# The projection of the values as seven products of halves instead of eight

## The chip, the cores and the metric

The kernel runs on one core of a Trainium2 chip. The core has a matrix engine (TensorE, PE in the profile), a vector engine (VectorE, DVE), an engine for activations and copies (ScalarE, ACT), a general one (GpSimd, POOL) and a queue for loads (SyncE, SP); POOL and ACT can issue transfers too. Each engine works off its own list of instructions in order and waits for the others by semaphores. The metric is the device time of one execution in microseconds; less is better.

## The reference

One layer of an encoder over 512 tokens of 1024 features, in float32. After a layer norm the tokens `h` are multiplied by one wide matrix `w_in`, whose columns give queries, keys and values of a 2-D neighbourhood attention (16 heads of 64), the inputs of a bidirectional state-space mixer (SSD), and two gates:

```
h = layer_norm(x)                         # 512 x 1024
proj = h @ w_in                           # columns: q | k | v | z | x,B,C | dt | gates
q, k, v, ... = split(proj)                # v: 512 x 1024, columns 2048..3071 of w_in
ya = neighbourhood_attention(q, k, v, rpb) @ w_attn_br   # 8 x 64 grid, window 8 x 16
ys = ssd(...) @ w_ssd_br
h = layer_norm(a * h + (sigmoid(g0) * ya + sigmoid(g1) * ys) @ w_o)
out = layer_norm(a * h + square(relu(h @ w_ff1)) @ w_ff2)
```

What is changed is how `v`, that is h (512 x 1024) times 1024 columns of w_in, is computed.

## The kernel before

**Products in float32.** Each float32 operand is kept as two parts, a high one (rounded to the matmul's format) and a low one (the remainder). `mm3` (L404 to L406) multiplies high by high, low by high and high by low, three matmuls for each 128 x 128 by 128 x 512 piece. Weights come in slabs of 1 MB (`ws`, loaded by SP, two buffers); ACT copies the high part (`wh`, L386), DVE subtracts for the low part (`wl`, L387), each in two halves of 128 x 1024, and `wh` and `wl` have two buffers each, too. The layer norm leaves the tokens as `hTh` and `hTl`, high and low, features on the partitions.

**Stages.** Layer norm and SSD come first; their order is laid out by a planner (class Plan), which assigns times and writes every engine's list out. Its last work is SSD branch 7: eight outputs `ps_sbr7_0` to `_7` in the two PSUM banks "mm", each emptied by DVE into the sum `ysacc` (L1104). From there on the order is set by the framework's scheduler, which places the instructions by the waits it sees. Then come the projection of the values, attention, the two branches with their gates, the output projection, and the FFN. The FFN's second matrix is multiplied with seven products of halves already; there POOL issues plain loads (L1559) and adding loads (L1570, a DMA that adds what it reads onto what lies in the slab).

**The projection of the values.** The tokens are first copied into another order, blocks of neighbourhood columns (`hBh`, `hBl`, 128 x 512 each, eight on ACT at L1186, eight on DVE at L1188). Then for each half of the 1024 columns (s) four PSUM banks, one for each block of 128 tokens, gather eight steps of 128 features: 2 x 4 x 8 x 3 = 192 matmuls of 128 x 512, over four slabs `ws_v`. The result leaves PSUM as high and low parts `vhl` (ACT L1202, DVE L1203).

**Attention** goes through eight pairs of heads. For each pair a slab `ws_qk` (two loads of 512 KB) is split, q and k are projected (`ps_q`, `ps_k`), copied out (`qf`, L1233; `kf`, L1246) and parted into `qs` (ACT L1238, POOL L1241), `kh` and `klz` (DVE L1249, POOL L1251). For each head eight small loads bring the relative biases (`raw`, L1262), which POOL turns into `bias` (L1267, L1271). Scores `pss` are added to the bias on DVE (`sc`, L1289), exponentiated on ACT (L1295), scaled (L1299), transposed on PE (`tp_p`, L1310) and multiplied with `vhl` (`po`, L1323). POOL also multiplies the gates `gt` with `ysacc` at the start of this stage (L1419).

## Time and profile before

| what | us |
|---|---|
| median of 3 runs (lowest, highest) | 1177.96 (1176.69, 1182.29) |
| the profiled execution | 1179.89 |
| its span, first to last instruction | 1178.1 |
| projection of the values on PE | 496.4 to 540.3 |
| PE busy | 1159.9 (98%) |
| DVE, ACT, POOL busy | 761.0, 615.0, 545.6 |
| mean granted clock of PE | 0.996 of full speed |

The profile is of one execution. A row of the timeline or of the chain of waits gives start, duration, engine, line, operation, output <- inputs, how many in a row, and in brackets the idle time before and what ended it. A row of a group of instructions gives the shortest, median and longest duration in ns, and the starts of the first and the last. A row of a stage gives busy time and count of each engine, then PE's granted clock, the mean busy share of the 16 DMA engines and what they moved in GB/s.

### The profile page before, as it was taken

To read this page: it belongs to the slowest core of one execution; us is meant where nothing else is said; L and a number is where in the kernel's file an instruction comes from. 1 tells how busy PE (TensorE), PEld (TensorE's weight loads), DVE (VectorE), ACT (ScalarE), POOL (GpSimd) and SP (SyncE) were. 2 spreads that over 40 slices of the span, in tenths; PEclk is the share of its full clock that TensorE was granted. 3 is DMA by queue.
4 is the path that set the end of the run, shared out by engine and by line. 5 is a ranking of instruction groups with operands and counts; after the bars stand their busy time and mean duration, and the time that the engine had idled before them with its cause. 6 is when DMAs were issued, how large, how long until landed. Compare 5 with 4: busy or idle time off the path is not lost.

```text
span 1178.1 us, 17062 instructions
## 1 busy us (share of the span) xinstructions
PE 1159.9 (98%) x6442; PEld 982.9 (83%) x6442; DVE 761.0 (65%) x1363; ACT 615.0 (52%) x1033; POOL 545.6 (46%) x588
## 2 busy tenths in 40 slices
PE   8999999999999999999999999999999999999997
PEld 8978797879888888888888888888988888878886
DVE  7757475676766665434788975556552666498856
ACT  6577583836365564524667773342263554365410
POOL 1168968778788767204667630016055131221000
PEclk9999999999999999999999999999999999999999
DMA  6353333333333342233423313543237986779511
GB/s 202 94 162 126 107 126 108 124 110 126 107 108 115 120 142 69 75 107 87 101 70 90 86 37 107 179 170 117 72 108 201 248 194 184 189 207 228 160 52 53
DMA packets 129409, 149.22 MB, mean 127 GB/s; under 512 B 22960, under 2 KB 101808, under 8 KB 129328
## 3 DMA queue, kind: packets, MB, share of 16 engines
q1 hardware_dynamic: 115696, 112.63, 30.8%
q0 software_dynamic: 13056, 34.61, 12.2%
q8 instruction: 50, 0.82, 0.3%
q10 hardware_dynamic: 576, 0.92, 0.2%
q14 instruction: 31, 0.25, 0.1%
HBM read 145.90 MB, written 2.23 MB: 126 GB/s over the span
## 4 chain that ended last, share of the span: by engine, by line
PE 83%; DMA 6%; DVE 5%; ACT 2%; issue 2%; POOL 2%; SPq 1%; DVEq 0%; POOLq 0%; ACTq 0%
PE ps_f L404 8%; PE ps_f L406 8%; PE ps_f L405 8%; PE ps_x L404 4%; PE ps_x L406 4%; PE ps_x L405 4%; PE ps_abr L1373 4%; PE ps_sbr L404 2%; DMA w2r<-in_w_ff 2%; PE ps_z L404 2%; PE ps_sbr L406 2%; PE ps_z L405 2%; PE ps_z L406 2%; PE ps_sbr L405 2%; PE ps_g L405 2%; PE ps_g L404 2%
## 5 line engine op out<-in xcount | busy, mean ns | idle before, releaser
L787 DVE SCALAR_TENSOR_TENSOR cv<-ps_x,pc,cv 128x511 f32<-128x511 f32 (+1 forms) x128 | 95.7, 748 | 24.7 <-ACT cv L779 21.4
L405 PE MATMUL ps_f<-h1Th,wl_f 128*128 128x512 f32 (+1 forms) x288 | 104.0, 365 | 0.0
L404 PE MATMUL ps_f<-h1Th,wh_f 128*128 128x512 f32 (+1 forms) x288 | 103.6, 365 | 0.0
L406 PE MATMUL ps_f<-h1Tl,wh_f 128*128 128x512 f32 (+1 forms) x288 | 102.0, 365 | 0.0
L1576 DVE TENSOR_TENSOR wl_f<-w2r,wh_f 128x1024 fp32r<-128x1024 f32 x42 | 49.9, 1221 | 64.4 <-ACT wh_f L1575 64.1
L404 PE MATMUL ps_z<-wh_z,hTh 128*128 128x256 f32 x256 | 75.2, 294 | 0.0
L405 PE MATMUL ps_z<-wh_z,hTl 128*128 128x256 f32 x256 | 71.5, 279 | 0.0
L406 PE MATMUL ps_z<-wl_z,hTh 128*128 128x256 f32 x256 | 71.5, 279 | 0.0
L1570 POOL DMA_DIRECT2D w2r<-in_w_ff x30 | 36.3, 1416 | 70.7 <-DMA w2r<-in_w_ff 45.7
L405 PE MATMUL ps_f<-wh_f,sql 128*128 128x512 f32 x168 | 65.3, 390 | 0.9 <-DVE sql L1576 0.9
L1575 ACT ACTIVATE wh_f<-w2r 128x1024 fp32r<-128x1024 f32 x42 | 42.6, 1052 | 44.0 <-DMA w2r<-in_w_ff 32.6
L404 PE MATMUL ps_f<-wh_f,sqh 128*128 128x512 f32 x168 | 65.3, 391 | 0.3 <-ACT sqh L1575 0.3
L406 PE MATMUL ps_f<-wl_f,sqh 128*128 128x512 f32 x168 | 65.3, 390 | 0.1
L1104 DVE TENSOR_TENSOR ysacc<-ps_sbr,ysacc 128x512 f32<-128x512 f32 x56 | 38.5, 689 | 37.5 <-PE ps_sbr L406 37.1
L404 PEld LDWEIGHTS ps_f<-h1Th,wh_f 128*128 128x128 f32 x288 | 53.9, 188 | 9.0
L405 PEld LDWEIGHTS ps_f<-h1Th,wl_f 128*128 128x128 f32 x288 | 53.9, 188 | 8.7
L387 DVE TENSOR_TENSOR wl_f<-ws_f,wh_f 128x1024 fp32r<-128x1024 f32 x36 | 47.2, 1348 | 20.5 <-ACT wh_f L386 20.4
L406 PEld LDWEIGHTS ps_f<-h1Tl,wh_f 128*128 128x128 f32 x288 | 52.8, 188 | 8.6
L404 PE MATMUL ps_x<-hTh,wh_bc 128*128 128x512 f32 (+1 forms) x144 | 56.7, 394 | 0.5 <-ACT hTh L614 0.5
L404 PE MATMUL ps_sbr<-yTh,wh_sbr 128*128 128x512 f32 x128 | 55.7, 435 | 0.7 <-ACT yTh L1081 0.4
L406 PE MATMUL ps_x<-hTl,wh_bc 128*128 128x512 f32 (+1 forms) x144 | 53.5, 371 | 1.9 <-DVE hTl L629 1.9
L404 PE MATMUL ps_x<-hTh,wh_x 128*128 128x512 f32 (+1 forms) x144 | 54.6, 379 | 0.0
(346 smaller groups left out, 3724.0 us busy)
## 6 DMA issues: line engine op xcount, KB each, us to landing
ws_f<-in_w_ff SPq DMA_DIRECT2D x20, 1024.0 KB
w2r<-in_w_ff POOLq DMA_DIRECT2D x18, 1024.0 KB, 7.9
bc<-acs_d SPq DMA_DIRECT2D x32, 512.0 KB
w2r<-in_w_ff POOLq DMA_DIRECT2D x30, 512.0 KB, 9.4
ws_bc<-in_w_in SPq DMA_DIRECT2D x16, 512.0 KB
ws_x<-in_w_in SPq DMA_DIRECT2D x8, 1024.0 KB
ws_z<-in_w_in SPq DMA_DIRECT2D x8, 1024.0 KB
ws_g<-in_w_in SPq DMA_DIRECT2D x8, 1024.0 KB
```

The costliest lines, as they stand in the source:

```text
L387: (eng[i] if isinstance(eng, tuple) else eng).tensor_tensor(out=lo[:, k], in0=st[:, k], in1=hi[:, k].bitcast(F32), op=ALU.subtract)
L404: nc.tensor.matmul(o, lh, rh, start=start, stop=False)
L405: nc.tensor.matmul(o, ll, rh, start=False, stop=False)
L406: return nc.tensor.matmul(o, lh, rl, start=False, stop=stop)
L787: op("DVE", 0.75, lambda j=j, o=o, n=n: nc.vector.scalar_tensor_tensor(out=acc()[:, o], in0=ps()[:, n], scalar=tap(j), in1=acc()[:, o], op ...
L1104: op("DVE", 0.69, lambda d=d, ps=ps: nc.vector.tensor_tensor(out=ysacc[:, d, :], in0=ps(), in1=ysacc[:, d, :], op=ALU.add), r=[(ps.name, 0 ...
L1373: ins.append(nc.tensor.matmul(pss[j], u, v, start=k + p == 0, stop=k == KD - 1 and p == 2))
L1570: nc.gpsimd.dma_start(t, rows(i, n, c, k), accum_op=ALU.add)
L1575: nc.scalar.activation(hi[:, k], x, AF.Copy)
L1576: low = nc.vector.tensor_tensor(out=lo[:, k], in0=x, in1=hi[:, k].bitcast(F32), op=ALU.subtract)
```

## The change

The tokens are cut into two halves i (the left and the right 32 columns of the 64-column grid) and two halves of the 1024 features; the weights into two halves of the features and two of the columns. Instead of eight products of such halves, seven are made, each of 256 tokens by 512 features by 512 columns: 2 x 4 x 3 = 24 matmuls of 128 x 512, 168 in all. They run in the order 1, 2, 5, 3, 6, 7, 4.

What they need is made on the chip. **Tokens:** POOL adds high and low parts of the four quarters (L1256 of the changed file), DVE forms the differences (L1268, L1283, L1285, L1300) in the memory of `aT`, and `tokens` parts them into high (ACT, L1217) and low (DVE, L1221), three buffers `vt`. **Weights:** the slab `ws_vsum` is loaded with block 01; adding DMAs of POOL (L1193, two of 512 KB each time) make 01 + 00, later + 11, later + 10, each time after the sum before has been split; block 01 is added onto `ws_v22`. SP loads four slabs as before; the adds read 4 MB more. **Results:** ACT copies the first product (L1278); the others are added on DVE (L1239, fourteen of 128 x 512), and ACT (L1246) and DVE (L1247) part them into `vhl`, now from SBUF. `behind` adds two explicit orderings. The copies hBh and hBl are gone. Everything that follows in the program text is the same.

```diff
 
     hb = tc.tile_pool(name="hb", bufs=1, reuse_waits="tile")
     hbp = hb.__enter__()
-    hBh = hbp.tile([P, KD, S], F32R, name="hBh")
-    hBl = hbp.tile([P, KD, S], F32R, name="hBl")
-    blk = "p (r b j) -> p b r j"
-    for k in range(KD):
-        for src, dst in ((hTh, hBh), (hTl, hBl)):
-            d4 = dst[:, k, :].rearrange("p (b r j) -> p b r j", r=8, b=4)
-            s4 = src[:, k, :].bitcast(F32).rearrange(blk, r=8, b=4)
-            if k < 4:
-                nc.scalar.activation(d4, s4, AF.Copy)
-            else:
-                nc.vector.tensor_copy(d4, s4)
-    for s in range(2):
-        pss = [psx.tile([P, 512], F32, tag=tag, bufs=BANKS[tag], name=f"ps_v{s}_{b}")
-               for b, tag in enumerate(("so", "tr", "so", "tr"))]
-        for k0 in (0, 4):
-            wv = weights([(w_in, k0 * P, OFF_V + s * 512, 512)], 4, 512, f"v{s}_{k0}")
-            for b in range(4):
-                bs = slice(b * P, (b + 1) * P)
-                for k in range(k0, k0 + 4):
-                    mm3(pss[b], hBh[:, k, bs], hBl[:, k, bs], wv[0][:, k - k0, :], wv[1][:, k - k0, :],
-                        k == 0, k == KD - 1)
-        for b in range(4):
-            pv4 = pss[b].rearrange("p (r h q) -> p r h q", r=4, h=2)
-            hi = vhl[s][:, b, :, 0:4:3, :]
-            vdone = nc.scalar.activation(hi, pv4, AF.Copy)
-            nc.vector.tensor_tensor(out=vhl[s][:, b, :, 1:3, :], in0=pv4, in1=hi.bitcast(F32),
-                                    op=ALU.subtract)
-
+
+    def project_values():
+        full = app.tile([P, 4, 4, 256], F32, tag="aT", name="v_full")
+
+        def block(i, n):
+            return w_in[i * 512 : (i + 1) * 512, OFF_V + n * 512 : OFF_V + (n + 1) * 512].rearrange(
+                "(k p) c -> p k c", p=P)
+
+        def load(name, i, n):
+            t = wp.tile([P, 4, 512], F32, tag="ws", name=f"ws_v{name}")
+            nc.sync.dma_start(t, block(i, n))
+            return t
+
+        def plus(t, i, n):
+            for k in (slice(0, 2), slice(2, 4)):
+                nc.gpsimd.dma_start(t[:, k], block(i, n)[:, k], accum_op=ALU.add)
+
+        def split(name, t, after=None):
+            hi, lo = [wide(wp.tile([P, 2112], F32R, tag=n, name=f"{n}_v{name}"), 4) for n in ("wh", "wl")]
+            for k in (slice(0, 2), slice(2, 4)):
+                x = nc.scalar.activation(hi[:, k], t[:, k], AF.Copy)
+                if after is not None:
+                    behind(x, after, "the tokens of the product before")
+                nc.vector.tensor_tensor(out=lo[:, k], in0=t[:, k], in1=hi[:, k].bitcast(F32),
+                                        op=ALU.subtract)
+            return hi, lo
+
+        def quarter(t, i, kk):
+            v = t[:, kk * 4 : kk * 4 + 4, :].bitcast(F32).rearrange("p k (r c) -> p k r c", r=8)
+            return v[:, :, :, i * 32 : i * 32 + 32]
+
+        high, low = {}, {}
+
+        def tokens(name, parts):
+            t = hbp.tile([P, 2, 4, 256], F32R, tag="vt", bufs=3, name=f"vt_{name}")
+            for b in range(2):
+                d = [t[:, n, :, b * P : (b + 1) * P].rearrange("p k (r j) -> p k r j", r=8)
+                     for n in range(2)]
+                hi, *rest = [x[:, :, :, b * 16 : b * 16 + 16] for x in parts]
+                done = nc.scalar.activation(d[0], hi, AF.Copy)
+                if rest:
+                    nc.scalar.activation(d[1], rest[0], AF.Copy)
+                else:
+                    low[name] = nc.vector.tensor_tensor(out=d[1], in0=hi, in1=d[0].bitcast(F32),
+                                                        op=ALU.subtract)
+            high[name] = done
+            return t
+
+        def product(pss, t, w):
+            for j in range(2):
+                for k in range(4):
+                    js = slice(j * P, (j + 1) * P)
+                    mm3(pss[j], t[:, 0, k, js], t[:, 1, k, js], w[0][:, k, :], w[1][:, k, :],
+                        k == 0, k == 3)
+
+        def two(name, *tags):
+            return [psx.tile([P, 512], F32, tag=tag, bufs=BANKS[tag], name=f"ps_v{name}_{j}")
+                    for j, tag in enumerate(tags)]
+
+        def add(out, x, pss, sign=1.0):
+            for j in range(2):
+                nc.vector.scalar_tensor_tensor(out=out[:, j], in0=pss[j], scalar=sign, in1=x[:, j],
+                                               op0=ALU.mult, op1=ALU.add if sign > 0 else ALU.subtract)
+
+        def values(s, half, src, after=None):
+            for j in range(2):
+                v4 = src[:, j].rearrange("p (r h q) -> p r h q", r=4, h=2)
+                hi = vhl[s][:, 2 * half + j, :, 0:4:3, :]
+                done = nc.scalar.activation(hi, v4, AF.Copy)
+                x = nc.vector.tensor_tensor(out=vhl[s][:, 2 * half + j, :, 1:3, :], in0=v4,
+                                            in1=hi.bitcast(F32), op=ALU.subtract)
+                if after is not None:
+                    behind(x, after, "the tokens of the product before")
+            return done
+
+        f21, f22, f11, f12 = [full[:, n].rearrange("p k (r c) -> p k r c", r=8) for n in range(4)]
+
+        def full_sum(f, i, kk):
+            return nc.gpsimd.tensor_tensor(out=f, in0=quarter(hTh, i, kk), in1=quarter(hTl, i, kk),
+                                           op=ALU.add)
+
+        full_sum(f22, 1, 1)
+        full_sum(f21, 1, 0)
+        w11 = load("11", 0, 0)
+        wsum = load("sum", 0, 1)
+        plus(wsum, 0, 0)
+        w21 = load("21", 1, 0)
+        t11 = tokens("11", [quarter(x, 0, 0) for x in (hTh, hTl)])
+        b11 = split("11", w11)
+        t12 = tokens("12", [quarter(x, 0, 1) for x in (hTh, hTl)])
+        nc.vector.tensor_tensor(out=f22, in0=f22, in1=f21, op=ALU.subtract)
+        s1 = tokens("s1", [f22])
+        full_sum(f11, 0, 0)
+        full_sum(f12, 0, 1)
+        p1 = two("1", "so", "so")
+        product(p1, t11, b11)
+        b21 = split("21", w21)
+        w22 = load("22", 1, 1)
+        sums = gep.tile([P, 2, 512], F32, tag="gt", bufs=4, name="v_sums")
+        for j in range(2):
+            nc.scalar.activation(sums[:, j], p1[j], AF.Copy)
+        p2 = two("2", "tr", "tr")
+        product(p2, t12, b21)
+        u1 = split("u1", wsum)
+        plus(wsum, 1, 1)
+        nc.vector.scalar_tensor_tensor(out=f22, in0=f22, scalar=-1.0, in1=f11, op0=ALU.mult,
+                                       op1=ALU.subtract)
+        nc.vector.scalar_tensor_tensor(out=f12, in0=f22, scalar=-1.0, in1=f12, op0=ALU.mult,
+                                       op1=ALU.subtract)
+        s4 = tokens("s4", [f12])
+        p5 = two("5", "mm", "mm")
+        product(p5, s1, u1)
+        b22 = split("22", w22)
+        plus(w22, 0, 1)
+        s2 = tokens("s2", [f22])
+        c11 = gep.tile([P, 2, 512], F32, tag="gt", bufs=4, name="v_c11")
+        add(c11, sums, p2)
+        u2 = split("u2", wsum, high["s4"])
+        plus(wsum, 1, 0)
+        p3 = two("3", "cb", "yd")
+        product(p3, s4, b22)
+        values(0, 0, c11, low["s4"])
+        nc.vector.tensor_tensor(out=f21, in0=f11, in1=f21, op=ALU.subtract)
+        s3 = tokens("s3", [f21])
+        u3 = split("u3", w22)
+        p6 = two("6", "so", "so")
+        product(p6, s2, u2)
+        t22 = tokens("22", [quarter(x, 1, 1) for x in (hTh, hTl)])
+        u4 = split("u4", wsum)
+        c12, c22 = [full[:, n].rearrange("p k c -> p (k c)").rearrange("p (j c) -> p j c", j=2)
+                    for n in (0, 3)]
+        add(sums, sums, p6)
+        add(c22, sums, p5)
+        add(c12, c22, p3, -1.0)
+        p7 = two("7", "tr", "tr")
+        product(p7, s3, u3)
+        values(1, 0, c12)
+        p4 = two("4", "so", "so")
+        product(p4, t22, u4)
+        add(c22, c22, p7, -1.0)
+        add(sums, sums, p7)
+        values(1, 1, c22)
+        add(sums, sums, p4)
+        return values(0, 1, sums)
+
+    vdone = project_values()
     hb.__exit__(None, None, None)
     at = tc.tile_pool(name="at", bufs=1, reuse_waits="tile")
     atp = at.__enter__()
```

The scheduler orders what follows the SSD anew. Three places are shown; the names after `<-` are the inputs, and a row with x2 stands for two of the kind in a row.

POOL from the last weight split of the SSD (`wl_sbr7`) on, before:

```order
L516 TENSOR_TENSOR wl_sbr7_4704<-ws_sbr7_4436,wh_sbr7_4695 128x1024 x2
L1213 MEMSET klz_5122 128x1024
L1419 TENSOR_TENSOR gt0_1_4748<-gt0_1_4748,ysacc_71 128x512 x2
L1267 TENSOR_TENSOR bias0_5224<-raw0_5215,cst_81 128x128
L1271 TENSOR_TENSOR bias0_5224<-raw0_5215,cst_81 128x128
L1267 TENSOR_TENSOR bias0_5224<-raw0_5215,cst_81 128x128
L1271 TENSOR_TENSOR bias0_5224<-raw0_5215,cst_81 128x128
L1241 TENSOR_TENSOR qs0_5160<-qf0_5158,qs0_5160 64x128 x3
```

and now:

```order
L516 TENSOR_TENSOR wl_sbr7_4704<-ws_sbr7_4436,wh_sbr7_4695 128x1024 x2
L1193 DMA ws_vsum_4857<-in_w_in 128x2x512 x2
L1256 TENSOR_TENSOR v_full_4852<-hTh_69,hTl_70 128x1024 x4
L1193 DMA ws_vsum_4857<-in_w_in 128x2x512 x2
L1193 DMA ws_v22_4919<-in_w_in 128x2x512 x2
L1193 DMA ws_vsum_4857<-in_w_in 128x2x512 x2
L1331 MEMSET klz_5174 128x1024
L1385 TENSOR_TENSOR bias0_5276<-raw0_5267,cst_81 128x128
L1389 TENSOR_TENSOR bias0_5276<-raw0_5267,cst_81 128x128
L1385 TENSOR_TENSOR bias0_5276<-raw0_5267,cst_81 128x128
L1389 TENSOR_TENSOR bias0_5276<-raw0_5267,cst_81 128x128
L1537 TENSOR_TENSOR gt0_1_4748<-gt0_1_4748,ysacc_71 128x512 x2
```

Between the last SSD split and the clearing of `klz` stand eight adding DMAs and four sums, and the first head's bias stands ahead of the two products with the gates instead of behind them.

DVE around the end of the SSD, where `ysacc` empties the last branch, before:

```order
L1104 TENSOR_TENSOR ysacc_71<-ps_sbr7_0_4772,ysacc_71 128x512
L387 TENSOR_TENSOR wl_v0_0_4875<-ws_v0_0_4876,wh_v0_0_4874 128x1024
L1104 TENSOR_TENSOR ysacc_71<-ps_sbr7_1_4780,ysacc_71 128x512
L387 TENSOR_TENSOR wl_v0_0_4875<-ws_v0_0_4876,wh_v0_0_4874 128x1024
L1104 TENSOR_TENSOR ysacc_71<-ps_sbr7_2_4788,ysacc_71 128x512
L1104 TENSOR_TENSOR ysacc_71<-ps_sbr7_3_4796,ysacc_71 128x512
L1104 TENSOR_TENSOR ysacc_71<-ps_sbr7_4_4804,ysacc_71 128x512
L1104 TENSOR_TENSOR ysacc_71<-ps_sbr7_5_4812,ysacc_71 128x512
L1104 TENSOR_TENSOR ysacc_71<-ps_sbr7_6_4820,ysacc_71 128x512
L1104 TENSOR_TENSOR ysacc_71<-ps_sbr7_7_4828,ysacc_71 128x512
L1188 CAST hBh_4852<-hTh_69 128x512
L1188 CAST hBl_4853<-hTl_70 128x512
```

and now:

```order
L1104 TENSOR_TENSOR ysacc_71<-ps_sbr7_0_4772,ysacc_71 128x512
L1201 TENSOR_TENSOR wl_v11_4869<-ws_v11_4855,wh_v11_4868 128x1024
L1104 TENSOR_TENSOR ysacc_71<-ps_sbr7_1_4780,ysacc_71 128x512
L1201 TENSOR_TENSOR wl_v11_4869<-ws_v11_4855,wh_v11_4868 128x1024
L1104 TENSOR_TENSOR ysacc_71<-ps_sbr7_2_4788,ysacc_71 128x512
L1104 TENSOR_TENSOR ysacc_71<-ps_sbr7_3_4796,ysacc_71 128x512
L1104 TENSOR_TENSOR ysacc_71<-ps_sbr7_4_4804,ysacc_71 128x512
L1104 TENSOR_TENSOR ysacc_71<-ps_sbr7_5_4812,ysacc_71 128x512
L1104 TENSOR_TENSOR ysacc_71<-ps_sbr7_6_4820,ysacc_71 128x512
L1104 TENSOR_TENSOR ysacc_71<-ps_sbr7_7_4828,ysacc_71 128x512
L1268 TENSOR_TENSOR v_full_4852<-v_full_4852 128x1024
L1201 TENSOR_TENSOR wl_v21_4914<-ws_v21_4861,wh_v21_4913 128x1024 x2
```

The two halves of the first slab's low part (`wl_v11` for `wl_v0_0`) stand at the same places between the evictions; behind them differences of tokens and the next split take the place of the copies.

SP from the loads of the q/k slabs on, before:

```order
L378 DMA ws_qk0_5126<-in_w_in 128x8x128 x2
L378 DMA ws_qk1_5371<-in_w_in 128x8x128 x2
L378 DMA ws_qk2_5616<-in_w_in 128x8x128 x2
L1262 DMA raw0_5215<-in_rpb_pad 16x8x32 x8
L1262 DMA raw1_5292<-in_rpb_pad 16x8x32 x8
L1262 DMA raw2_5460<-in_rpb_pad 16x8x32 x8
L378 DMA ws_qk3_5861<-in_w_in 128x8x128 x2
```

and now:

```order
L378 DMA ws_qk0_5178<-in_w_in 128x8x128 x2
L378 DMA ws_qk1_5423<-in_w_in 128x8x128 x2
L378 DMA ws_qk2_5668<-in_w_in 128x8x128
L1380 DMA raw0_5267<-in_rpb_pad 16x8x32 x8
L1380 DMA raw1_5344<-in_rpb_pad 16x8x32 x8
L1380 DMA raw2_5512<-in_rpb_pad 16x8x32 x8
L378 DMA ws_qk2_5668<-in_w_in 128x8x128
L378 DMA ws_qk3_5913<-in_w_in 128x8x128 x2
```

The second half of `ws_qk2` has moved behind the 24 loads of `raw`.

## The prediction

> **What bounds the kernel now.** I read the page's table of engines first, then the busy time by stage, the instructions of the projection, and the chain of waits where that stage begins.
>
> ```profile
> span 1178.1 us, 17062 instructions
> PE 1159.9 (98%) x6442; PEld 982.9 (83%) x6442; DVE 761.0 (65%) x1363; ACT 615.0 (52%) x1033; POOL 545.6 (46%) x588
> ...
> core 0: us, PE busy (x) PEld busy (x) DVE busy (x) ACT busy (x) POOL busy (x), PEclk, DMA share, GB/s
> 485.00:496.40 11.40, 11.33 (x50) 8.89 (x49) 6.92 (x9) 6.75 (x11) 0.00 (x0) 1.00 0.29 93
> 496.40:540.30 43.90, 43.90 (x195) 36.38 (x194) 17.38 (x24) 12.34 (x16) 0.00 (x0) 1.00 0.33 96
> ...
> L404 PE MATMUL ps_v<-wh_v,hBh x64: 389/389/389, 496.6 to 539.4; 128*128 128x512 f32 x64
> L406 PE MATMUL ps_v<-wl_v,hBh x64: 389/389/389, 497.7 to 539.9; 128*128 128x512 f32 x64
> ```
>
> TensorE (PE) is busy for 98% of the span, and in the projection (496.4 to 540.3) for all of it at the full granted clock, while POOL does nothing, DVE 17.4 us and the DMA engines a third of what they could. The stage is 192 matmuls in a row. So a matmul less is a gain of its whole pitch, and anything that makes PE wait is a loss of its whole length: there is no slack on PE to hide it in. What lies just ahead of the stage is the place that matters here:
>
> ```profile
> 486.78 0.69 DVE L1104 TENSOR_TENSOR ysacc<-ps_sbr,ysacc 128x512 f32<-128x512 f32 x1 [5.82 <-PE ps_sbr L406]
> 487.39 1.22 DVE L387 TENSOR_TENSOR wl_v<-ws_v,wh_v 128x1024 fp32r<-128x1024 f32 x1
> 488.52 0.69 DVE L1104 TENSOR_TENSOR ysacc<-ps_sbr,ysacc 128x512 f32<-128x512 f32 x1
> 489.12 1.22 DVE L387 TENSOR_TENSOR wl_v<-ws_v,wh_v 128x1024 fp32r<-128x1024 f32 x1
> 490.25 1.40 DVE L1104 TENSOR_TENSOR ysacc<-ps_sbr,ysacc 128x512 f32<-128x512 f32 x2
> ...
> 490.25 0.69 DVE ysacc L1104
> 490.99 0.50 PE ps_sbr L404
> ```
>
> The last SSD branch (eight outputs through two PSUM banks) is emptied by DVE, and the first two halves of the V weights' low parts stand between those evictions in DVE's queue. In the chain (the last two rows) PE's fifth output starts at 490.99, right behind the eviction of the third (490.25 + 0.69): PE already waits for DVE there. Whatever delays DVE between 487 and 491 goes on the path at once.
>
> **The change part by part.** *Fewer matmuls.* 192 become 168. The pitch, from the first matmul of L404 to the last of L406, is (539.9 - 496.6) / 191 = 0.2267 us. 24 x 0.2267 = **-5.44 us**. That is 0.46% of 1178, and nothing else is removed from the path, so 5.4 is the most that the change can bring.
>
> *POOL gets work where it had none, beside DVE.* In the new order POOL goes, behind its last weight split, to two adding DMAs (weight block 00 onto 01) and then to four sums hTh + hTl of 128x1024 (L1256 of the changed file). When?
>
> ```profile
> 474.77 4.75 POOL L516 TENSOR_TENSOR wl_sbr<-ws_sbr,wh_sbr 128x1024 fp32r<-128x1024 f32 x2 [0.98 <-ACT wh_sbr L512]
> 540.38 0.95 POOL L1213 MEMSET klz<- 128x1024 f32 x1 [60.87 <-PE ps_v L406]
> 479.54 11.19 SPq L378 DMA_DIRECT2D ws_v<-in_w_in  x2
> 483.00:484.00 1.00, 1.00 (x6) 0.84 (x5) 0.00 (x0) 0.00 (x0) 0.00 (x0) 1.00 0.85 330
> 484.00:485.00 1.00, 1.00 (x7) 0.81 (x6) 0.00 (x0) 0.00 (x0) 0.00 (x0) 1.00 0.02 6
> L1570 POOL DMA_DIRECT2D w2r<-in_w_ff x30: 1177/1228/1729, 896.3 to 1084.6; - x30
> DMA to landing us min/median/max: 6.0/9.4/18.0
> L516 POOL TENSOR_TENSOR wl_z<-ws_z,wh_z x16: 2375/2406/2417, 42.1 to 433.3; 128x1024 fp32r<-128x1024 f32 x16
> L1104 DVE TENSOR_TENSOR ysacc<-ps_sbr,ysacc x56: 673/692/693, 177.9 to 496.8; 128x512 f32<-128x512 f32 x56
> ```
>
> POOL is free from 479.5. The slab that is added onto takes the place of today's second V slab: issued at 479.54, its bytes stop at about 484.2 (330 GB/s in the second before 484, then 6). Two issues of 1.23 us each (the FFN's adding DMAs, L1570) bring POOL to 486.7, and the four sums, 2.4 us each by L516, fill 486.7 to 496.3: exactly the stretch of the DVE rows above. Do the two engines disturb each other? The nearest case is in the FFN:
>
> ```profile
> 867.74 22.81 POOL L1700 TENSOR_TENSOR acc<-acc,row 128x1024 f32<-128x1024 f32 x8 [53.49 <-ACT r L1683]
> 869.84 4.72 DVE L387 TENSOR_TENSOR wl_f<-ws_f,wh_f 128x1024 fp32r<-128x1024 f32 x2 [1.97 <-ACT wh_f L386]
> ```
>
> Two DVE subtractions of the shape of wl_v took 4.72 us beside POOL's additions, where each wl_v above takes 1.22; and POOL's eight took 22.8 where 8 x 2.41 = 19.3. So both lose, and the loss is about the other's work. The evictions ysacc, whose one input is PSUM, never took over 0.693 us in 56 cases, many of them beside POOL's splits: they aren't touched. Taken as turns, an operation waiting until the other engine's is through: POOL's first sum 486.7 to 489.1; the first wl_v (wanted 487.4) 489.1 to 490.3; the eviction of the second output 490.3 to 490.9; POOL's second sum starts at 490.3 behind wl_v and lasts to 492.7; the second wl_v 492.7 to 493.9; the eviction of the third output to 494.6 instead of 490.94. PE's fifth output, and all behind it, starts **+3.6 us** later. If they only shared the rate, each wl_v would last twice as long, 2 x 1.2 = +2.4. Bounds: 0, if the two don't meet (the slab lands over 5 us later, or the sums are short), and 4.8, two whole sums. I take 3.6, since the rows show waiting of about that kind.
>
> [...]
>
> *The adding DMAs.* Eight of 512 KB, in pairs. Call T the start of the first product on PE; a product is 24 x 0.2267 = 5.44 us, and they run 1, 2, 5, 3, 6, 7, 4. The second add (block 11) can start when the sum slab's first split is done, about T + 7.9; its result is wanted by product 6 at T + 21.8. The third (block 10) waits for the next split of that slab, which stands on DVE behind the tokens of products 3, 2 and 7: about T + 21.5, and product 4 wants it at T + 32.7, less one ACT half (1.05) and the start of it: a landing within 9.8 us costs nothing. The add onto 22 has T + 13.1 to T + 27.2. The FFN's adds landed after 6.0 to 18.0 us, median 9.4, at a DMA share far above the 0.33 of this stage; there the first half of a pair is near the minimum. I take **0**, with bounds 0 and what 18 us would give (rival C).
>
> *DVE's load.* From T to the low part of the first q/k weights it has 18 operations of 128x1024 and 21 of 128x512. By the starts above (487.39 to 488.52, 488.52 to 489.12) these follow at 1.13 and 0.60: 20.3 + 12.6 = 32.9 us, against 168 x 0.2267 = 38.1 us of PE. It fits, with 5 us to spare; before, DVE was busy for 17.4 us of 43.9. ACT has less. **0**, bounds 0 and 2 for a late operand.
>
> *The handover to attention.* Two orders change: on SP the second half of ws_qk2 now stands behind the 24 small loads of raw, and on POOL the first bias stands ahead of the two gt multiplications.
>
> ```profile
> 540.07 12.29 SPq L1262 DMA_DIRECT2D raw<-in_rpb_pad  x24
> 552.46 6.53 SPq L378 DMA_DIRECT2D ws_qk<-in_w_in  x4
> 546.86 0.46 POOL L1267 TENSOR_TENSOR bias<-raw,cst 128x128 f32<-128x128 f32 x1 [0.93 <-DMA raw<-in_rpb_pad]
> 548.66 4.21 POOL L1241 TENSOR_TENSOR qs<-qf,qs 64x128 fp32r<-64x128 f32 x10
> 551.81 2.01 ACT L386 ACTIVATE wh_qk<-ws_qk 128x1024 fp32r<-128x1024 f32 x2
> 558.48 0.42 DVE L1289 CUSTOM_DVE_ANT_0 sc<-pss,bias 128x256 f32<-128x256 f32 x1 [0.51 <-PE pss L1285]
> 562.51 1.14 DVE L1299 TENSOR_SCALAR sc<-sc,sums 128x256 f32<-128x256 f32 x4
> 566.88 0.77 PE tp_p L1310 x7
> ```
>
> The first softmax is ready at 563.65 and PE transposes it at 566.88: 3.2 us of slack. After the change raw goes out some 2.3 us later measured from the end of the projection, the 12.3 us of its issues stand ahead of half a q/k slab, so ACT's wh_qk and the eviction behind it come 4 to 6.7 us later and the first score 3.3 us later; PE has, by the new order, five more q matmuls (5 x 0.2267 = 1.1 us) ahead of the transpose. 3.3 against 3.2 + 1.1 leaves nothing or a little: **+0.5**, bounds 0 and 3 (if PE, which waits for ACT here already, can't fill with q).
>
> Sum: -5.44 + 3.6 + 0 + 0 + 0.5 = **-1.3 us**. The profiled execution took 1179.89 (span 1178.1 and 1.8 around it), so it would take 1178.6; it lies 1.9 over the median of the runs, 1177.96, which would become **1176.6**.
>
> **Rivals.** *B, the whole gain.* The sums and DVE's splits don't meet: 1177.96 - 5.44 + 0 to 0.5 = 1172.5 to 1173. For it: the slab's landing is only known to a microsecond or so, and a part of DVE's wait may be there already. Against it: the 4.72 us row, and that the sums last 9.6 us in a stretch of which DVE's splits need the first four.
>
> *C, slower: the add on block 10 comes late.* If a pair lands as the FFN's first four did, up to the 18.0 us of the row, say 10 for the first half and 15 for the second: block 11's second half goes out at T + 9.1, lands at T + 24.3, and is split by T + 26.6 (1.05 + 1.22) instead of the T + 23.6 at which its first low part is wanted, 3.0 us of waiting; block 10's goes out 3.0 late at T + 25.7, lands at T + 40.7, split at T + 43.0 against T + 34.5 + 3.0: 5.5 more. 1176.6 + 8.5 = 1185.1. It decides from a second half's landing of about 10 us. For it: the median of 9.4 lies just under that point, and the q/k slabs load at the same time. Against: 4 MB in 40 us beside a share of 0.33, and pairs alone.
>
> *D, the handover costs 3:* -5.44 + 3.6 + 3 = +1.2, 1179.1. For it, the q/k weights behind 24 loads; against, the slack of 3.2.
>
> **How the numbers follow.** A (the sum) 0.50; B 0.24; C 0.13; D 0.13. What a measurement of this kernel can tell from no change is about 0.5%, 5.9 us: below 1172.1 is faster, above 1183.9 slower. A and D lie within it. B lies half a microsecond inside, and the runs before spread over 1176.69 to 1182.29, so four in ten of B count as faster, and a little of A: 0.11. C counts as slower nearly whole, with a little of D: 0.14. Same 0.75. The range takes B from 1172.0 and reaches up to 1183.0, half way from D to C, since C's price grows steadily with the landing.
>
> **What would show it.** (1) ps_v: 168 matmuls, 0.2267 apart, if no wait lies between; a row of PE waiting for ACT or DVE behind an add's landing is C. (2) The two wl_v11 rows (L1201) between the ysacc rows: 2.4 us and more from the ysacc before to their end, the first ps_v matmul about 500.2; at 496.6, B. (3) L1256: four operations of 2.4 us, stretched by about 1.2 each for the first two. (4) The first score's start against the projection's end, 18.2 us before (558.48 - 540.3): 21.5 forecast; PE's wait ahead of tp_p. The prediction is wrong if T moves by less than 1 or over 5 us, or if PE waits over 1 us between products.

## The result: slower, and the loss lies ahead of the projection

The changed kernel takes 1185.71 us (median of six runs, 1183.77 to 1188.03), the kernel before 1178.22 on the same chip: a ratio of 1.0061 with a 95% interval of 1.0047 to 1.0074, some 7 us more. Forecast were 1176.6, with a range up to 1183.0. The profiled execution of the changed kernel took 1185.6 us with a span of 1183.6.

The page of the changed kernel, its list of what PE waited for between 480 and 760, and the first group of matmuls of the projection and its last one:

```profile
span 1183.6 us, 17096 instructions
PE 1156.8 (98%) x6418; PEld 981.5 (83%) x6418; DVE 791.4 (67%) x1387; ACT 627.9 (53%) x1053; POOL 564.2 (48%) x600
...
PE ps_sbr L404 <- DVE ysacc L1104: 9.4, 1, 9.4
PE tp_p L1428 <- DVE sc L1417: 1.5, 1, 1.5
PE po L1441 <- ACT qf L1351: 0.4, 1, 0.4
...
L404 PE MATMUL ps_v<-wh_v,vt x16: 389/389/389, 507.8 to 518.0; 128*128 128x512 f32 x16
...
545.68 0.39 PE L406 MATMUL ps_v<-wl_vu,vt 128*128 128x512 f32 x1
```

Three things are to be seen. The projection begins at 507.8 instead of 496.6. Its last matmul starts at 545.7 and takes 0.39 us, so it ends at 546.1 instead of 540.3 and lasts 38.2 us instead of 43.7: it does bring what it was to bring. And in it PE waits for nothing: both waits of any size lie outside, one before it (9.4 us, for an eviction of the last SSD branch), one in attention. What happened ahead of it stands in the timelines of POOL and of DVE:

```profile
485.06 2.63 POOL L1193 DMA_DIRECT2D ws_vsum<-in_w_in  x2 [5.73 <-DMA ws_vsum<-in_w_in]
486.80 10.13 POOL L1256 TENSOR_TENSOR v_full<-hTh,hTl 128x1024 f32<-128x1024 f32 x4
...
486.59 0.69 DVE L1104 TENSOR_TENSOR ysacc<-ps_sbr,ysacc 128x512 f32<-128x512 f32 x1 [5.82 <-PE ps_sbr L406]
487.20 10.82 DVE L1201 TENSOR_TENSOR wl_v<-ws_v,wh_v 128x1024 fp32r<-128x1024 f32 x1
497.94 0.68 DVE L1104 TENSOR_TENSOR ysacc<-ps_sbr,ysacc 128x512 f32<-128x512 f32 x1
498.54 1.21 DVE L1201 TENSOR_TENSOR wl_v<-ws_v,wh_v 128x1024 fp32r<-128x1024 f32 x1
```

One subtraction of DVE takes 10.82 us instead of 1.22. It began 0.4 us behind the first of POOL's four sums and ended 1.1 us, about its own length, behind the last (486.80 + 10.13 = 496.93). The eviction queued behind it came 9.6 us late, measured from the eviction before it. The second wl_v, with POOL done, took 1.21 again. What PE lost besides is in the granted clock, the last number but two of each row (the columns are as in the prediction's table by stage):

```profile
487.20:498.60 11.40, 2.07 (x10) 1.38 (x8) 11.40 (x4) 4.77 (x9) 9.72 (x5) 0.76 0.54 93
498.60:503.70 5.10, 5.03 (x12) 3.98 (x13) 2.44 (x4) 0.00 (x0) 0.00 (x0) 0.53 0.55 169
503.70:507.80 4.10, 4.10 (x19) 3.38 (x18) 2.08 (x3) 0.00 (x0) 0.00 (x0) 1.00 0.12 45
508.00:546.20 38.20, 38.20 (x170) 31.62 (x170) 34.55 (x41) 24.35 (x33) 7.25 (x7) 1.00 0.78 165
```

Behind the wait PE ran at about half its clock: 12 matmuls in the 5.1 us after 498.6, which at 0.2267 us each would be 2.7. So 9.4 of waiting and 2.4 of low clock, less some 0.5 us that PE lost at this place before the change too (48 matmuls in 11.36 us, which at 0.2267 would be 10.88), make up the 11.4 us by which the projection starts late.

To compare profiles, whose earlier stages differ by a microsecond or two, I take the first eviction of branch 7 as zero (486.78 before, 486.59 after). The first matmul of the projection then comes at 9.8 before and 21.2 after, and the first of the next stage, ps_abr, at 209.9 and 218.2. So the loss is 8.3 us by the end of attention: +11.4 ahead of the projection, -5.4 in it, and 2.3 in attention. In this pair of profiles the rest gave 2.6 of it back (first before, then changed):

```profile
L1373 PE MATMUL ps_abr<-aTh,wh_abr x64: 389/389/398, 696.7 to 742.8; 128*128 128x512 f32 x64
L404 PE MATMUL ps_f<-h1Th,wh_f x288: 276/389/395, 832.0 to 1120.2; 128*128 128x512 f32 x112, 128*128 128x256 f32 x32
```

```profile
L1491 PE MATMUL ps_abr<-aTh,wh_abr x64: 389/389/397, 704.8 to 750.8; 128*128 128x512 f32 x64
L404 PE MATMUL ps_f<-h1Th,wh_f x288: 276/389/395, 840.1 to 1125.7; 128*128 128x512 f32 x112, 128*128 128x256 f32 x32
```

From ps_abr to the last ps_f of this line it is 423.5 us before and 420.9 after, though nothing was changed in the program text there; in the runs below it is 421 to 426. In the profile of before PE waits 1.2 us for operands of the FFN (ps_f) that it does not wait for in the changed kernel's; how much of the rest is variation from one execution to another, a single profile of each does not show. So spans of single profiles are not compared here to less than 3 us.

### The profile page after: what moved, and what is told of

Read it like the earlier page. It is cut to its first block, busy times and chain, and to the rows that moved or that the text cites. A ratio compares the mean times of both kernels' runs of the same rounds, so it can differ in the third digit from the quotient of the medians.

```text
span 1183.6 us, 17096 instructions
## 1 busy us (share of the span) xinstructions
PE 1156.8 (98%) x6418; PEld 981.5 (83%) x6418; DVE 791.4 (67%) x1387; ACT 627.9 (53%) x1053; POOL 564.2 (48%) x600
## 4 chain that ended last, share of the span: by engine, by line
PE 84%; DVE 5%; DMA 4%; ACT 2%; issue 2%; SPq 1%; POOL 1%; DVEq 0%; ACTq 0%; POOLq 0%
PE ps_f L404 9%; PE ps_f L405 9%; PE ps_f L406 9%; PE ps_x L404 4%; PE ps_x L406 4%; PE ps_x L405 4%; PE ps_abr L1491 4%; PE ps_sbr L404 2%; PE ps_sbr L406 2%; PE ps_z L404 2%; PE ps_sbr L405 2%; PE ps_z L405 2%; PE ps_z L406 2%; PE ps_g L405 2%; PE ps_g L404 2%
## 5 line engine op out<-in xcount | busy, mean ns | idle before, releaser
L1104 DVE TENSOR_TENSOR ysacc<-ps_sbr,ysacc 128x512 f32<-128x512 f32 x56 | 38.5, 688 | 39.4 <-PE ps_sbr L406 39.1
```

The costliest lines, as they stand in the source:

```text
L1104: op("DVE", 0.69, lambda d=d, ps=ps: nc.vector.tensor_tensor(out=ysacc[:, d, :], in0=ps(), in1=ysacc[:, d, :], op=ALU.add), r=[(ps.name, 0 ...
```

## The experiments

Eleven kernels ran. The first question was whether the sums on POOL or the adding DMAs ahead of them held DVE up, and by what rule; the second, whether attention's loss can be had back. The table has the times from the first eviction of branch 7 as above. The kernels ran on several chips, on which the kernel before took 1178.2 to 1178.9 us (1180.4, one run, on that of e12).

| kernel | first ps_v | first ps_abr | time, us |
|---|---|---|---|
| before | 9.8 | 209.9 | 1178.2 |
| changed | 21.2 | 218.2 | 1185.7 |
| changed, waits between the sums (e2) | 21.3 | 216.7 | 1184.7, one run |
| changed, a wait ahead of the first sum (e12) | 21.0 | 219.3 | 1187.6, one run |
| changed, only two sums at the place (e3) | 17.1 | 212.2 | 1180.4, one run |
| before, with the four sums (e4) | 15.3 | 215.5 | 1185.2, one run |
| changed, sums ahead of the adds (e6) | 13.4 | 218.7 | 1192.9, one run |
| changed, sums behind the first wl_v11 (e8) | 11.6 | 207.1 | 1176.4, one run |
| changed, sums behind the second wl_v11 (e1) | 9.8 | 208.5 | 1175.7 |
| the same, ws_qk2 ahead of raw, two ways (e5, e9) | 9.8, 9.8 | 214.0, 213.8 | 1187.4, 1185.3 |
| the same, the first scores ahead of wl_qk2 (e11) | 9.8 | 209.5 | 1181.1, one run |
| changed, two sums early, two behind (e10) | 9.8 | 208.6 | 1174.7 |

**Moving the sums (e1).** `low["w11"]` is the second half of wl_v11; the same call stands at all four sums.

```diff
-        full_sum(f22, 1, 1)
-        full_sum(f21, 1, 0)
...
+        behind(full_sum(f22, 1, 1), low["w11"], "the split of the first slab")
+        behind(full_sum(f21, 1, 0), low["w11"], "the split of the first slab")
...
-        full_sum(f11, 0, 0)
-        full_sum(f12, 0, 1)
+        behind(full_sum(f11, 0, 0), low["w11"], "the split of the first slab")
+        behind(full_sum(f12, 0, 1), low["w11"], "the split of the first slab")
```

> The changed kernel with one difference: the four sums of tokens on POOL stand behind the second wl_v11 on DVE, so that they run from about 490.4 on, beside evictions from PSUM. Theory W (the four sums, which follow each other on POOL without a wait, keep DVE's subtraction out until the last is through): wl_v11 takes 1.2 us again, the first ps_v matmul is back at 496.6 instead of 507.8, the projection ends at about 535, and with the 2 us that the start of attention lost the time is 1178.2 - 5.4 + 2 = 1174 to 1176. Rival S (the two adding DMAs ahead of the sums hold DVE up, not the sums): wl_v11 still takes some 10 us and the time stays at 1185.

The order of all other instructions stayed as in the changed kernel. Median 1175.73 of ten runs, ratio to the kernel before 0.9976 (0.9961 to 0.9991). From its timelines:

```profile
492.43 10.45 POOL L1256 TENSOR_TENSOR v_full<-hTh,hTl 128x1024 f32<-128x1024 f32 x4 [2.78 <-DVE wl_v L1201]
...
489.39 1.22 DVE L1201 TENSOR_TENSOR wl_v<-ws_v,wh_v 128x1024 fp32r<-128x1024 f32 x1
```

Moving four instructions turns the loss of 7 us into a gain of 2.4 (by the medians on its chip, 1178.15 and 1175.73). The adds still stood ahead of wl_v11, so they alone do not hold DVE up. The fourth sum, in its new place, meets the next subtraction (wl_v21, 3.41 us), and the projection lasts 39.1 us.

**The price alone (e4).** The kernel before, with four sums that nobody reads, started by the first half of wh_v (`split_weights.first`); no adds.

```diff
+            if not s and not k0:
+                for i in range(4):
...
+                    behind(nc.gpsimd.tensor_tensor(out=full[:, i].rearrange("p k (r c) -> p k r c", r=8),
+                                                   in0=quarter[0], in1=quarter[1], op=ALU.add),
+                           split_weights.first, "the first half of the slab")
```

> The kernel before with the price alone: POOL makes the four sums hTh + hTl (nobody reads them) behind the first half of wh_v, no adding DMA, no other part of the change. Theory W and rival N: the first wl_v waits until all four are through (about 497 instead of 488.6), PE stands for 9 us and then runs at a lower granted clock for some us; first ps_v matmul about 507.5 instead of 496.6, time about 1178 + 11 = 1189. Rival S: no adds, so no stall, 1178.

Both theories missed. POOL's first sum again stands a fraction of a microsecond ahead of DVE's subtraction, but the engines now take turns:

```profile
487.81 11.33 POOL L1202 TENSOR_TENSOR v_full<-hTh,hTl 128x1024 f32<-128x1024 f32 x4 [7.62 <-ACT wh_v L386]
...
488.07 3.22 DVE L389 TENSOR_TENSOR wl_v<-ws_v,wh_v 128x1024 fp32r<-128x1024 f32 x1
...
491.81 2.78 DVE L389 TENSOR_TENSOR wl_v<-ws_v,wh_v 128x1024 fp32r<-128x1024 f32 x1
...
493.00:498.00 5.00, 4.19 (x11) 2.80 (x10) 2.79 (x3) 0.00 (x0) 5.00 (x3) 0.50 0.41 125
```

The subtractions take 3.22 and 2.78 us: each waits for one sum, and POOL's four sums last 11.33 instead of 4 x 2.41 = 9.6. The projection starts 5.5 us late: the prediction's 3.6 for turns, by which the third eviction ends late, and 1.9 for the half clock that followed (the last row: 11 matmuls in 4.2 us).

**Waits between the sums (e2), two sums (e3), a wait ahead of the first (e12).** These keep the place and ask what makes DVE wait for the whole run. In e2 `copies` are ACT's first copies of the tokens.

```diff
+        behind(full_sum(f21, 1, 0), copies[0], "a copy")
...
+        behind(full_sum(f11, 0, 0), copies[2], "a copy")
+        behind(full_sum(f12, 0, 1), copies[3], "a copy")
```

> The changed kernel; the second, third and fourth sum on POOL now wait each for one more copy of ACT that is done about when they start (487.7 to 490), so the order and the place are unchanged but the sums no longer stand in one run without waits. Theory W: DVE gets in between the first and the second sum; the first wl_v11 ends near 490.3, the second near 493.9, the first ps_v matmul comes at about 500 to 501, the time is about 1178. Rival N (POOL goes first whenever it has work, wait or not): wl_v11 ends behind the fourth sum as in the changed kernel, first ps_v matmul 507.8, time 1185.7.

```profile
486.69 10.14 POOL L1257 TENSOR_TENSOR v_full<-hTh,hTl 128x1024 f32<-128x1024 f32 x4
...
487.27 10.66 DVE L1201 TENSOR_TENSOR wl_v<-ws_v,wh_v 128x1024 fp32r<-128x1024 f32 x1
```

So it is not that the sums stand in one run without waits written between them: my first theory fell. The test is weaker than it looks, since each copy was done before its sum came up (the second sum starts at 489.05, its copy had ended at 488.41), so POOL never paused. What speaks against the theory more plainly is e4, where the sums follow each other without a pause, too, and DVE gets in between. In e3 the first two sums are left at their place and the other two carry e1's call.

> The changed kernel, two of the four sums left at their place right behind the adding DMAs, the other two behind the second wl_v11. If the wait is for the whole run of sums, the first wl_v11 takes 4.6 us + 1.2 = about 5.9 us (instead of 10.8), the first ps_v matmul comes 5 to 7 us later than before and the time is about 1180. If the wait has a length of its own (a time-out, the landing of the adds), it stays near 10 us.

```profile
486.90 5.57 POOL L1256 TENSOR_TENSOR v_full<-hTh,hTl 128x1024 f32<-128x1024 f32 x2
...
487.33 6.23 DVE L1201 TENSOR_TENSOR wl_v<-ws_v,wh_v 128x1024 fp32r<-128x1024 f32 x1
```

6.23 us with two sums, 10.82 with four: DVE waits for as many as there are. In e12 the first sum gets a wait for a slab that had landed long before, since in all runs with turns the first sum stood behind some wait:

```diff
-        full_sum(f22, 1, 1)
+        w11 = load("11", 0, 0)
+        behind(full_sum(f22, 1, 1), loads["11"], "the first slab")
         full_sum(f21, 1, 0)
-        w11 = load("11", 0, 0)
```

> The changed kernel, order and place unchanged, but the first of the four sums waits for the landing of the first slab (w11), which came some 10 us earlier: a wait that is satisfied long before. In the runs in which the engines took turns the first sum had stood behind a wait of its own (ACT's wh_v11 or DVE's wl_v11), so it is open whether the wait or the end of the DMA issue makes the difference. Theory D (the first sum starts while POOL is still issuing the adding DMA): the sum still starts some 0.9 us before the end of the issue, and the first wl_v11 takes over 10 us, time about 1185. Rival V (a wait ahead of the first sum is enough): wl_v11 about 3.2 and 2.8 us, first ps_v matmul 5 us later than before instead of 11, time about 1179.

```profile
485.61 2.63 POOL L1193 DMA_DIRECT2D ws_vsum<-in_w_in  x2 [5.50 <-DMA ws_vsum<-in_w_in]
487.34 10.13 POOL L1256 TENSOR_TENSOR v_full<-hTh,hTl 128x1024 f32<-128x1024 f32 x4
...
487.98 10.58 DVE L1201 TENSOR_TENSOR wl_v<-ws_v,wh_v 128x1024 fp32r<-128x1024 f32 x1
```

The sum starts at 487.34, 0.9 us before POOL's second DMA issue ends (485.61 + 2.63 = 488.24), as in the changed kernel (486.80 against 487.69), and DVE waits for all four.

**The adds behind the sums (e6), the sums once the issue is over (e8).** In e6 the sums start with the first half of wh_v11 and `plus(wsum, 0, 0)` follows them; e8 is e1 with the first half of wl_v11 in place of the second, so the adds are issued but still under way.

```diff
+        for f, i, kk in ((f22, 1, 1), (f21, 1, 0), (f11, 0, 0), (f12, 0, 1)):
+            x = full_sum(f, i, kk)
+            behind(x, high["w11"], "the first half of the first slab")
+        plus(wsum, 0, 0, x)
```

> The changed kernel with POOL's order turned round: the four sums first (from the end of the first half of wh_v11 on), the two adding DMAs behind them. The scheduler also orders attention anew, so only the start of the projection is read. Theory D (DVE is kept out for the whole run of sums only where the first of them starts while POOL is still issuing a DMA ahead of it; else the engines take turns): wl_v11 takes about 3.2 and 2.8 us as in the kernel before with sums alone, the first ps_v matmul comes 5 us later than before, not 11. Rival A (what differs is something else in the changed program): the first wl_v11 takes over 9 us again.

> The changed kernel, the four sums behind the first half of wl_v11 instead of the second: POOL has issued both adding DMAs by then, but they are still under way (a landing takes 6 to 9 us). Theory D: turns; the second wl_v11 waits for one sum and takes 2.5 to 3.6 us, PE waits some 2.5 us. Rival F (adds in flight are enough): the second wl_v11 waits until the fourth sum is through, about 10 us, and the first ps_v matmul comes 11 us late.

First e6 (with one row of what PE waited for), then e8:

```profile
488.93 11.39 POOL L1260 TENSOR_TENSOR v_full<-hTh,hTl 128x1024 f32<-128x1024 f32 x4 [7.62 <-ACT wh_v L1200]
...
489.19 3.23 DVE L1204 TENSOR_TENSOR wl_v<-ws_v,wh_v 128x1024 fp32r<-128x1024 f32 x1
...
PE ps_v L404 <- ACT wh_vu L1200: 4.2, 2, 2.5
```

```profile
485.56 2.63 POOL L1193 DMA_DIRECT2D ws_vsum<-in_w_in  x2 [5.62 <-DMA ws_vsum<-in_w_in]
489.13 10.39 POOL L1256 TENSOR_TENSOR v_full<-hTh,hTl 128x1024 f32<-128x1024 f32 x4 [0.94 <-DVE wl_v L1201]
...
489.55 3.05 DVE L1201 TENSOR_TENSOR wl_v<-ws_v,wh_v 128x1024 fp32r<-128x1024 f32 x1
```

Turns in both. In e6 the projection starts 13.4 - 9.8 = 3.6 us late, with the clock at full speed; e6 is the slowest of all for what comes later. Its adds go out at 500.65, some 14 us later measured from the first eviction; PE then waits 4.2 us for what is split from them, with 3.4 us at half clock, and the projection lasts 44.5 us instead of 38.2. The order of attention is a new one, too. In e8 the first sum starts 0.9 us after the DMA issue is over (488.19), with the adds' data still under way.

Put together: in four programs (changed, e2, e3, e12) the first sum starts before POOL's DMA issue ahead of it has ended, and DVE waits for the whole run of sums; in three (e4, e6, e8) it starts with no issue going on, and the two engines take turns. The number of sums, waits that are already satisfied and data under way do not decide which of the two happens. An issue alone does not hold DVE up either: in e8 the first wl_v11 starts at 487.82, before the issue ends, and takes 1.22 us.

The sums one by one show how the two cases differ, first in the changed kernel, then in e8:

```profile
L1256 POOL TENSOR_TENSOR v_full<-hTh,hTl x4: 3178/3206/3303, 486.8 to 493.7; 128x1024 f32<-128x1024 f32 x4
```

```profile
L1256 POOL TENSOR_TENSOR v_full<-hTh,hTl x4: 2385/2388/3345, 489.1 to 497.1; 128x1024 f32<-128x1024 f32 x4
```

In the changed kernel each sum takes 3.2 us and the next starts 2.3 us after it. So each starts 0.9 us before the one ahead of it has ended, as the first starts 0.9 us before the end of the issue, and no moment without a sum is left between them. It is the same in e2, in e12 and in the two early sums of e3. In e4, e6 and e8 a sum starts 0.03 to 0.06 us before the end of the one ahead; those that met no subtraction took 2.4 us. That this overlap, begun by the issue, is what keeps DVE out is my reading of it; the runs show the condition and the overlap, not the mechanism.

Two things were not tried: plain loads of POOL in place of adding ones, and a first sum that follows other work of POOL without a pause and without an issue. Against the pause as the cause speaks e4, where the second wl_v gets in between the second and the third sum, which have no pause between them.

**Attention (e5, e9, e11).** All three are e1 with one edit. In e5 the raw loads of the first two heads wait for one of DVE's last operations of the projection; in e9 the loads of ws_qk2 have priority; in e11 wl_qk2 stands behind the first scores.

At the loads of raw (e5), at the loads of the q/k slabs (e9), and at their low parts (e11):

```diff
+                if h < 2:
+                    behind(d, vlow[1, 1, 0], "the weights of the third pair")
```

```diff
+            with tc.high_priority() if name == "qk2" else ExitStack():
```

```diff
+            if name == "qk2":
+                tc.add_manual_dep(y.ins, first_score[0].ins.name, mybir.DependencyInfo(
+                    mybir.DependencyClass.NoSync, mybir.DependencyReason.DATA), reason="the first scores")
```

> As the run with the sums behind wl_v11, and the loads of raw for the first two heads wait for one of DVE's last operations of the projection, so that SP issues the second half of ws_qk2 ahead of them again. If the 2.1 us that attention lost are those of ws_qk2's second half behind the 24 loads: the first score comes about 18.5 us behind the end of the projection instead of 21, PE has no wait ahead of tp_p, and the time is 2 us under the run without it, 1172 to 1174. If the loss came from POOL (bias ahead of gt) or ACT, it stays.

> As the run with the sums behind the second wl_v11, and the two loads of ws_qk2 have priority on SP over the 24 of raw; the scheduler then orders the rest of attention anew. If those loads are what attention lost: no wait of PE ahead of the first tp_p and 1172 to 1174. If the order that the scheduler finds for the rest decides, as in the first try at this (1187, with waits of PE for po later on), the first wait is gone and others come, 1176 to 1187.

> The run with all four sums behind the second wl_v11; on DVE the third pair's low parts (wl_qk2) are put behind the first head's scores instead of ahead of them, so that the first softmax no longer waits for the late half of ws_qk2. The scheduler orders the later heads anew. If that late half is what makes PE wait for the first tp_p: the first score comes about 18 us behind the end of the projection instead of 22, and there is no wait and no lower clock at the first tp_p. The total shows what the new order of the rest costs; from the first eviction of branch 7 to the first ps_abr matmul 208.5 us would be as without this edit, 206 the gain.

In each, SP's or DVE's order became the wanted one, and in each the scheduler ordered the rest of attention anew. What PE waits for in e9:

```profile
PE po L1442 <- DVE aT L1456: 4.5, 2, 3.4
PE po L1443 <- DVE ptl L1434: 2.2, 1, 2.2
...
PE tp_p L1429 <- DVE sc L1418: 0.2, 1, 0.2
```

The wait ahead of tp_p is down to 0.2 us, as expected if ws_qk2's late half was its cause; but other waits (6.7 us for po, with the clock at 0.50 for 3.4 us in two places behind them) took its place, in e5 the same ones. The first score came 20.3 us behind the end of the projection in e5, where 18.5 was expected, and the times are 1187.39 (ratio 1.0075, 1.0051 to 1.0099) and 1185.31 (1.0059, 1.0043 to 1.0076). In e11 the first score came 19.5 us behind the end of the projection instead of 22.2 in e1 (18 was expected); a wait of 0.9 us for tp_p remained, and one of 1.6 for po came. None isolates the one loss: that would take attention's order held fixed, which wasn't tried.

**Two sums early (e10).** POOL stood idle from 479.4 until the sum slab landed; two sums go there, ahead of the adds, and two behind the second wl_v11.

```diff
-        full_sum(f21, 1, 0)
+        two_sums = full_sum(f21, 1, 0)
...
+        with tc.issue_after(two_sums.ins):
+            plus(wsum, 0, 0)
...
+        behind(full_sum(f11, 0, 0), low["w11"], "the split of the first slab")
+        behind(full_sum(f12, 0, 1), low["w11"], "the split of the first slab")
```

> The changed kernel with two of the four sums on POOL ahead of the first adding DMAs (from about 479.4 to 484.2, where POOL stood idle until the sum slab had landed) and the other two behind the second wl_v11; no sum starts beside an issue of a DMA, none meets a wl_v11. Expected: wl_v11 1.2 us each, the first ps_v matmul 9.8 us behind the start of the first eviction of branch 7 as before (496.6 - 486.78), the projection in 38.1 us without the 0.8 us that the run with all four behind wl_v11 lost at the fourth product, and attention's 2 to 3 us still lost: 1174 to 1175.5. [...]

```profile
478.89 4.77 POOL L1256 TENSOR_TENSOR v_full<-hTh,hTl 128x1024 f32<-128x1024 f32 x2
484.57 2.63 POOL L1193 DMA_DIRECT2D ws_vsum<-in_w_in  x2 [0.91 <-DMA ws_vsum<-in_w_in]
489.85 4.75 POOL L1256 TENSOR_TENSOR v_full<-hTh,hTl 128x1024 f32<-128x1024 f32 x2 [2.65 <-DVE wl_v L1201]
...
PE tp_p L1429 <- DVE sc L1418: 1.5, 1, 1.5
```

1174.72 (median of twelve), ratio 0.9967 (0.9954 to 0.998): 3.9 us faster than the kernel before; its interval overlaps that of e1, so which of the two is faster stays open. No wl_v11 meets a sum, and the projection lasts 38.7 us, 5.0 less than before. Attention takes 3.7 us longer than before (the last row is its first wait), so that 1.3 of the 5.0 are left at ps_abr; the rest of the measured 3.9 lies behind it, where the profile of before is 2.5 us longer than this one.

## Why the prediction was wrong, point by point

**What bounds the kernel, and the fewer matmuls: right.** PE is busy for 98% of the span, and the projection shrank by 5.4 us in the changed kernel and by 5.0 in e10 (forecast 5.44). The stretch of DVE's queue between 487 and 491 was the place that decided.

**POOL's work beside DVE: the step that failed.** Place, time and cause were right: the sums start at 486.80 (forecast 486.7), are through after 10.13 us (forecast 9.6), and the subtraction wl_v11 behind the first eviction is what they hit. The price was not. "Taken as turns, an operation waiting until the other engine's is through" gave +3.6, with 4.8, two whole sums, as the upper bound; measured were 11.4. Two parts were missed. First, the turns themselves: they were read from the FFN's row (4.72 us for two subtractions beside POOL's additions), where POOL issues no DMA just ahead of its additions (53.49 us of idleness stand there). Where no issue is going on the reading holds to the tenth (e6: 3.6; e4: 3.6 before the clock); here the sums follow a DMA issue that is still going on (it ends at 487.69, the first sum starts at 486.80), and DVE waits for all four. No row of the profile of before shows that case, and the bound should have been the whole run of sums, 4 x 2.4 = 9.6, since the nearest row differed in just what the change adds. Second, the clock: a wait of PE was priced at its own length, and the half clock behind it cost 2.4 us more (1.9 in e4).

In the turns of e4, e6 and e8 a subtraction of 1.22 us beside a sum of 2.4 took 3.22, 3.23 and 3.05 us: it waited for one sum at most. In the changed kernel and in e3, with 10.82 and 6.23 us, the wait outlasted four sums and two.

The granted clock was 0.50 for 3.4 us (585.3 to 588.7 in the changed kernel), 6.8 (492.5 to 499.3 in e4) or 10.2 (493.2 to 503.4 in the changed kernel, from within the wait of 9.4 us on). How long a wait was did not settle whether it came: single waits of 1.5 us (tp_p in the changed kernel) and 1.8 (e4) were followed by it, and so were three of 0.9 us and less in e1, 1.9 in all; waits of 1.8 in e6 and of 1.9 in e8 were not. What settles it, the runs do not show.

**The adding DMAs: right, and with them rival C's mechanism wrong.** Over the whole projection PE waited for no sum of weights.

```profile
L1193 POOL DMA_DIRECT2D ws_vsum<-in_w_in x6: 1197/1292/1667, 485.1 to 530.7; - x6
DMA to landing us min/median/max: 6.0/7.9/8.7
```

They landed within 8.7 us, under the 9.8 that the prediction allowed. Rival C had 1185.1, and 1185.7 was measured, but by another way: the time agreed, the cause did not, and only the list of PE's waits tells the two apart. That late adds do cost time is seen in e6, where PE waited 4.2 us for what is split from them; C had put 8.5 on it. (By C's own terms block 11 lands at T + 24.1, not T + 24.3, which changes its price by about 0.2.)

**DVE's load: right.** In the projection it was busy for 34.6 of 38.2 us (forecast 32.9 up to the first q/k weights), without holding PE up.

**The handover: right in direction, a size off.** Forecast +0.5 (0 to 3), measured 2.3. The chain of the changed kernel goes the way that was named:

```profile
560.00 3.91 DMA ws_qk<-in_w_in
563.99 1.07 ACT wh_qk L386
565.08 0.98 DVE wl_qk L387
...
567.44 0.34 DVE sc L1407
...
577.51 2.20 DVE wl_qk L387
...
582.42 1.47 DVE sc L1417
583.88 0.14 issue
584.02 1.24 PE tp_p L1428 x8
```

The half of ws_qk2 behind the 24 loads of raw lands at 563.9, and the first score follows at 567.4, 21.3 us behind the end of the projection (forecast 21.5). The first head's transposes were still in time; the delay shows at the second head's, at 584.0, where PE waits 1.5 us and then, once more, runs at half clock, for 3.4 us: up to 1.7 us that the forecast had no term for. (The slack was also a little less than the prediction read: its row of seven transposes at 566.88 has one more ahead of it at 566.38, so that it was 2.7 us, not 3.2.)

How much goes with the clock is seen in the programs whose order of instructions is that of the changed kernel throughout. From the end of the projection to the first ps_abr the kernel before took 156.4 us. Two whose clock was 1.00 from 560 to 600, where the first heads wait, took 156.9 (e3) and 157.2 (e8), so 0.5 and 0.8 more, about the forecast 0.5. Two with 3.4 us at 0.50 there (585.3 to 588.7 in the changed kernel, 577.3 to 580.7 in e1) took 158.7 (changed) and 159.6 (e1), so 2.3 and 3.2 more. The half clock itself explains at most 1.7 of that; the rest is open. e2 took 157.2 and e12 160.1, at a mean clock of 0.993 and 0.990 over the whole execution (the changed kernel: 0.991).

## What to carry to other kernels

When work is moved onto an idle engine, look at which of its instructions run beside which of another engine's, and take as the upper price not one instruction but the whole run of them (here 10.82 us beside four sums); a row that shows the two engines side by side counts only if what stands ahead of the run is the same, too. Where PE is the bound, price a wait of a few microseconds with the lower clock behind it as well (here 9.4 us of waiting and 2.4 more). And before a good idea is dropped, try its pieces in another order: here the same 168 matmuls were 7 us slower or 4 us faster than before, by where four additions stood.

## What the runs showed of the hardware

- A run of GpSimd additions that started while the same engine was still issuing a DMA (0.9 us before the issue ended) kept a VectorE subtraction with two SBUF operands out until its last addition had ended: 10.6 to 10.8 us for four (changed, e2, e12), 6.2 for two (e3), where it took 1.2 alone. Each addition then started 0.9 us before the one ahead had ended. Without an issue going on the two engines took turns, 2.8 to 3.4 us for a subtraction (e1, e4, e6, e8).
- VectorE's additions that read PSUM kept 0.68 to 0.69 us beside the same sums (e1, e8).
- Behind single waits of PE of 1.5 to 9.4 us, and behind three of 0.9 us and less in e1, the granted clock was often, not always, 0.50, for 3.4, 6.8 or 10.2 us; ahead of the projection that cost 2.4 us in the changed kernel and 1.9 in e4. A wait of 1.9 us in e8 and two of 1.8 and 1.7 in e6 left it at 1.00.
- Small changes of the order at one place made the scheduler order all of attention anew, by up to 5.5 us up to the next stage (208.5 against 214.0); such a version has to be measured as a whole.
